# A two-layer hybrid decoder step on one core: a denser samples' chain, 64 expert blocks beside the gates instead of 72, and the last four expert blocks' products regrouped

## The chip, the cores and the metric

One core of one Trainium2 chip runs the whole program as a single launch. The metric is the device time of one execution in microseconds (us). Before the change the median of three runs is 3731.05 us (3728.86 to 3739.23).

## The reference, cut to what matters

Two trunk layers run over 512 prompt tokens (one sequence) and 64 sample tokens (8 sequences of 8), 1024 channels wide, in float32. Each layer has a mixer (a projection to 6 x 1024 columns, a gated recurrence, a short convolution, an output projection) and then an expert stage, in which every token takes 8 heads x 16 experts out of 16384.

```python
def trunk_layer(x, c, ...):
    sh1, sc1, g1, sh2, sc2, g2 = jnp.split(c @ w_ada + b_ada, 6, axis=-1)
    proj = modulate(rmsnorm(x, norm1), sh1, sc1) @ w_in
    ...
    merged = jax.nn.sigmoid(ga) * ya + jax.nn.sigmoid(gb) * yb
    x = x + g1[:, None, :] * (merged @ w_out)
    hn2 = modulate(rmsnorm(x, norm2), sh2, sc2)
    x = x + g2[:, None, :] * peer(hn2, ...)

def peer(...):                        # per block of tokens
    s = jnp.einsum('thpd,hpkd->thpk', q, sub_keys)
    sv, si = lax.top_k(s, TOPK)
    ...                               # 16 x 16 candidates, top 16 again: idx, g
    act = jax.nn.gelu(jnp.einsum('thkd,td->thk', u_tab[idx], xb))
    return jnp.einsum('thk,thkd->td', g * act, v_tab[idx])
```

## The kernel before, in words

**Two ways through the experts.** The first 384 prompt tokens (`TD`) go dense: the kernel multiplies them with all 16384 rows of the u table and of the v table, in 128 blocks of 128 experts, with a gate matrix that is zero where a token did not choose an expert. The other 128 prompt tokens (two groups of 64) and the 64 samples go by gathers: one indirect load on POOL brings 128 table rows (512 KB) at a time, and VectorE (DVE) either takes a dot product (`udot`, L666) or adds a weighted row (`vsum`, L682). These gathers are tasks in a queue (`gtasks`), 130 for the samples and 259 for the prompt tokens in each layer. `pump(n)` (L157) takes n of them, as a running credit, and is called from the loops of the dense work; what is left after the last block is flushed at L1052.

**Every dense float32 product is split.** `split_blk` (L127) makes a high part on ScalarE (ACT, L132) and a low part on DVE (L133, `lo_...`), and TensorE (PE) does three products. The split tiles rotate through 4 buffers (`HIS`), the raw blocks of 512 KB through 6 (`RAWS`); loads are issued by SP.

**A layer's stages.**
- The mixer (`mixer_in`, L334) does 48 projections of 24 products (`pj`, L150). Beside each, `beside()` (L369) takes `SIDE` steps of the samples' chain: the 64 samples' own pass through the same mixer, the query and the top-16 choice, a generator (`samples`, L459) of 56 steps, 36 of which load 1 MB (`sa_...`, L475). In layer 0 it also takes one chunk of the conditioning (`ada`, 1 MB, `pm`). When the chain has ended, `beside` pumps `MPUMP` gathers a projection.
- The output projection (`po`), then the queries (`pq`, with the top-16 choices on DVE, 8 heads).
- `phase_a` (L926): the products of the u blocks 0 to `NA`-1 (`u_mm`, `pu`, L713, 24 of 384 columns a block), beside the 96 pieces of the gate matrix (`oh` L945 and `A` L950 on DVE, `pgm` L955 on PE, eviction on ACT, 24 stores to DRAM). Blocks below `NS_` spill their activations to DRAM, the last 16 stay on the chip. In layer 0 the conditioning of layer 1 (24 chunks) goes here too.
- `phase_b` (L992): the blocks from `NA` on first, each with its u product just ahead (`meet`, `UAHEAD` pairs early; the stage is called the meets here), then the 16 resident ones, then the spilled ones (called the rest). For each block the activations are multiplied with the gates, split, and 18 products of 512 columns go to six PSUM banks (`pvo`, L1016). Six copies to SBUF (`ys`, L1059), transposes (`pyt`, L1065) and the update of x end the layer.

Nobody writes the order of the instructions by hand: a scheduler with a timeline of its own lays them out, by the priorities that `tc.high_priority` and `tc.issue_after` give.

## Time and profile before

| what | value |
|---|---|
| median of 3 runs | 3731.05 us |
| the profiled execution | 3730.17 us, span 3728.4 us |
| PE / DVE / ACT / POOL busy | 94% / 79% / 40% / 30% |
| granted PE clock, mean | 0.96 |
| DMA | 1032.70 MB, mean 277 GB/s |
| instructions | 52710 |

Layer 0 runs to about 1932 us of the span and layer 1 from there to the end. The table of stretches further down (rows 2) is cut at the stage ends. Busy time of PE is an upper bound, since a matmul that waits in the pipeline counts as busy. The pace of the products is therefore taken from the distance between starts.

### The profile page before, as it was taken

The page shows a single profiled execution, that of the slowest core. Times are in us where ns is not written, and L with a number is a line of the kernel's source. Part 1 is how long each engine was busy: PE and PEld are TensorE (multiplying, and loading weights), DVE is VectorE, ACT ScalarE, POOL GpSimd, SP SyncE. Part 2 cuts the span into 40 slices and gives each one's busy share as a digit, 9 for nine tenths or more (in the row PEclk, how much of TensorE's full clock was granted, in tenths as well). Part 3 has the DMA queues.
Part 4 walks back from the last instruction along what each step waited for, and adds up shares of the span by engine and source line. Part 5 has one row for each costly group of instructions (what it writes and reads, how often), then busy time and mean ns, then how long its engine had stood idle before and what let it go on. Part 6 is the DMA issues. An engine that isn't in the chain of part 4 may idle for free.

```text
span 3728.4 us, 52710 instructions
## 1 busy us (share of the span) xinstructions
PE 3501.1 (94%) x18606; PEld 2910.8 (78%) x18606; DVE 2961.9 (79%) x6160; ACT 1481.8 (40%) x2027; POOL 1119.1 (30%) x830
## 2 busy tenths in 40 slices
PE   7999989989999999999959999899999999999996
PEld 4447768977789999988844576789987999998885
DVE  5338889998758888888873489899998788888887
ACT  3324343435553333333323344434456433333332
POOL 0001530052004444432320036200720355554422
PEclk9999989989999999999979999999987999999998
DMA  8775853479879999999856669524984899999994
GB/s 296 269 253 202 303 201 111 157 267 348 325 272 322 342 340 339 336 366 347 323 186 231 247 214 332 173 89 173 336 310 187 289 347 338 343 337 363 357 336 169
DMA packets 393449, 1032.70 MB, mean 277 GB/s; under 512 B 54240, under 2 KB 159840, under 8 KB 386400
## 3 DMA queue, kind: packets, MB, share of 16 engines
q1 hardware_dynamic: 267616, 554.28, 42.6%
q0 software_dynamic: 110592, 402.70, 29.8%
q10 hardware_dynamic: 14976, 72.36, 4.8%
q8 instruction: 146, 2.39, 0.2%
q14 instruction: 119, 0.97, 0.1%
HBM read 954.01 MB, written 75.15 MB: 276 GB/s over the span
## 4 chain that ended last, share of the span: by engine, by line
PE 59%; issue 17%; POOL 11%; DVE 6%; DMA 5%; ACT 2%; POOLq 0%; SPq 0%; ACTq 0%; DVEq 0%
PE pu L713 22%; PE pvo L1016 14%; PE pj L150 8%; PE pq L871 5%; POOL vrp L660 4%; POOL urp L660 4%; POOL urs L660 3%; PE po L150 2%; PE pgm L955 1%; DMA raw_wi<-in_win_dram 1%; DVE A L950 1%; DVE oh L945 1%; PE pm L186 1%; DMA vrp<-in_vtab_dram,gidx 1%; DMA raw_ada<-in_wada_dram 1%
## 5 line engine op out<-in xcount | busy, mean ns | idle before, releaser
L660 POOL DMA_INDIRECT urp<-in_utab_dram,gidx x256 | 370.8, 1448 | 558.1 <-DVE dot L666 435.2
L660 POOL DMA_INDIRECT vrp<-in_vtab_dram,gidx x256 | 352.5, 1377 | 491.9 <-DVE accp L682 457.6
L1016 PE MATMUL pvo<-hi_v,h2h 128*128 128x512 f32 x1536 | 485.4, 390 | 0.0
L1016 PE MATMUL pvo<-lo_v,h2h 128*128 128x512 f32 x1536 | 476.8, 389 | 0.0
L1016 PE MATMUL pvo<-hi_v,h2l 128*128 128x512 f32 x1536 | 461.7, 389 | 0.0
L660 POOL DMA_INDIRECT vrs<-in_vtab_dram,gidxs x128 | 217.8, 1702 | 789.1 <-DVE fid L786 373.4
L713 PE MATMUL pu<-h2h,hi_u 128*128 128x384 f32 x1152 | 397.7, 345 | 4.8 <-ACT hi_u L132 3.3
L713 PE MATMUL pu<-h2h,lo_u 128*128 128x384 f32 x1152 | 395.2, 343 | 2.3 <-DVE lo_u L133 2.3
L713 PE MATMUL pu<-h2l,hi_u 128*128 128x384 f32 x1152 | 395.7, 343 | 0.0
L660 POOL DMA_INDIRECT urs<-in_utab_dram,gidxs x128 | 171.8, 1342 | 670.2 <-issue 314.3
L133 DVE TENSOR_TENSOR lo_v<-raw_v,hi_v 128x1024 fp32r<-128x1024 f32 x256 | 312.9, 1222 | 54.9 <-ACT hi_v L132 48.0
L150 PE MATMUL pj<-hnh,hi_wi 128*128 128x512 f32 (+1 forms) x800 | 320.7, 402 | 33.2 <-ACT hi_wi L132 12.8
L1016 PEld LDWEIGHTS pvo<-lo_v,h2h 128*128 128x128 f32 x1536 | 288.3, 188 | 60.8
L1016 PEld LDWEIGHTS pvo<-hi_v,h2l 128*128 128x128 f32 x1536 | 288.3, 188 | 60.5
L682 DVE SCALAR_TENSOR_TENSOR accp<-vrp,dot,accp 128x1024 f32<-128x1024 f32 x252 | 322.7, 1280 | 12.0 <-DMA vrp<-in_vtab_dram,gidx 10.8
L1016 PEld LDWEIGHTS pvo<-hi_v,h2h 128*128 128x128 f32 x1536 | 287.3, 188 | 56.1
L150 PE MATMUL pj<-hnl,hi_wi 128*128 128x512 f32 (+1 forms) x800 | 314.6, 393 | 4.2 <-DVE hnl L281 4.2
L150 PE MATMUL pj<-hnh,lo_wi 128*128 128x512 f32 (+1 forms) x800 | 316.3, 396 | 1.9 <-DVE lo_wi L133 1.8
L666 DVE CUSTOM_DVE_ANT_0 urp<-urp,xt 128x1024 f32<-128x1024 f32 x256 | 306.0, 1219 | 1.7 <-DMA urp<-in_utab_dram,gidx 1.6
L713 PE MATMUL pu<-h2h,lo_ub 128*128 128x384 f32 x896 | 300.1, 335 | 0.0
L713 PE MATMUL pu<-h2h,hi_ub 128*128 128x384 f32 x896 | 299.9, 335 | 0.0
L713 PE MATMUL pu<-h2l,hi_ub 128*128 128x384 f32 x896 | 299.7, 334 | 0.0
(439 smaller groups left out, 7178.4 us busy)
## 6 DMA issues: line engine op xcount, KB each, us to landing
raw_v<-in_vtab_dram SPq DMA_DIRECT2D x256, 512.0 KB
raw_u<-in_uT_dram SPq DMA_DIRECT2D x144, 512.0 KB
raw_ub<-in_uT_dram SPq DMA_DIRECT2D x112, 512.0 KB
raw_wi<-in_win_dram SPq DMA_DIRECT2D x96, 512.0 KB
gd<-stg ACTq DMA_DIRECT2D x48, 1024.0 KB
gt<-gd SPq DMA_DIRECT2D x768, 64.0 KB
raw_ada<-in_wada_dram SPq DMA_DIRECT2D x86, 512.0 KB
ad<-ao ACTq DMA_DIRECT2D x56, 384.0 KB
```

The costliest lines, as they stand in the source:

```text
L133: anchor[0] = V.tensor_tensor(out=lo, in0=raw, in1=hi.bitcast(F32), op=ALU.subtract).ins
L150: PE.matmul(out[:, c0:c1], a[:, w], b[:, k, c0:c1], start=(k == 0 and a is hi and b is xh), stop=(k == KT - 1 and a is lo))
L186: PE.matmul(pm[j * 32:(j + 1) * 32, 0:256], c32[:, k, :], raw[k // 4][:, j * 256:(j + 1) * 256], start=(k < 4), stop=(k >= 4))
L660: G.indirect_dma_start(out=rt, out_offset=None, in_=tab, in_offset=bass.IndirectOffsetOnAxis(ap=self.gidx[:, g, h, k:k + 1], axis=0))
L666: V.tensor_tensor_reduce(out=ur, in0=ur, in1=self.xt[g], scale=1.0, scalar=0.0, op0=ALU.mult, op1=ALU.add, accum_out=self.dot[:, g, h, k:k ...
L682: V.scalar_tensor_tensor(out=self.acc[g], in0=vr, scalar=w, in1=self.acc[g], op0=ALU.mult, op1=ALU.add)
L713: ends[i] = PE.matmul(pu[:, 0:TD], a[:, w], b[:, 0:NT, k, :], start=(k == 0 and a is hi and b is h2h), stop=(k == KT - 1 and a is lo)).ins
L871: PE.matmul(pqs[:, t0 * P:t1 * P], a[:, w], b[:, t0:t1, k, :], start=(k == 0 and a is hi and b is h2h), stop=(k == KT - 1 and a is lo))
L945: V.tensor_tensor(out=o, in0=iota2.unsqueeze(1).to_broadcast([P, 2, P, 2]), in1=slot(t, a, c0), op=ALU.is_equal)
L950: V.tensor_tensor(out=A[:, z], in0=oh[0], in1=slot(t, 2 + z, c0), op=ALU.mult)
L955: PE.matmul(pgm[:, n * P:(n + 1) * P], oh[1][:, n // 2, :, n % 2], A[:, z, n // 2, :, n % 2], start=(z == 0), stop=(z == 1))
L1016: PE.matmul(pv[t][q], a[:, tk], b[:, q * 512:(q + 1) * 512], start=(n == 0 and a is wh and b is vh), stop=(n == P - 1 and a is wl))
```

## The change

Four constants change, and two pieces of code. `NA` goes from 72 to 64, so that 64 u blocks run beside the gates and 64 in the meets (the resident ones are now 48 to 63, and 24 pairs are spilled, not 28). `SIDE` goes from (3.0, 3.5) to (4.5, 6.0) steps a projection, `MPUMP` from 2.5 to 2.6, and `BPUMP` from 3.0 and 1.0 to 3.2 and 1.4 gathers a block. `beside` takes two chunks of the conditioning at a time; its added condition `c < KT - 0` always holds. The products of the last two pairs (four blocks) are held back and issued after the loop, one 128-token tile `t` after the other, each followed by its copy out; the last pair's weights go to a part of `h2h`/`h2l` that is free by then.

```diff
-NA = 72
+NA = 64
...
-SIDE = (3.0, 3.5)
-MPUMP, QRATE, ARATE, BPUMP = 2.5, 0.0, 0.3, (3.0, 1.0)
+SIDE = (4.5, 6.0)
+MPUMP, QRATE, ARATE, BPUMP = 2.6, 0.0, 0.3, (3.2, 1.4)
...
-            if todo:
-                ada(l, [todo.pop(0)])
+            for _ in range(2):
+                if todo:
+                    ada(l, [todo.pop(0)])
...
-            if steps[0] < -1.0:
+            if steps[0] < -1.0 and c < KT - 0:
                 pump(MPUMP)
...
+        whe, wle = (h_[:, 0, :, :].rearrange("p k t -> p (k t)") for h_ in (h2h, h2l))
+        held = []
...
-                wh, wl = (w_[:, u * TD:(u + 1) * TD] for w_ in (wht, wlt))
+                last = n == P // 2 - 1
+                wh, wl = (w_[:, u * TD:(u + 1) * TD] for w_ in ((whe, wle) if last else (wht, wlt)))
...
-                for t in range(NT):
-                    products(t, 2 * n + u, wh, wl, vh, vl)
+                if n >= P // 2 - 2:
+                    held.append((2 * n + u, wh, wl, vh, vl))
+                else:
+                    for t in range(NT):
+                        products(t, 2 * n + u, wh, wl, vh, vl)
...
         for t in range(NT):
+            for h_ in held:
+                products(t, *h_)
             yt = ys[:, t].rearrange("p k t -> p (k t)")
```

**Place 1, the end of layer 0.** DVE before, from the next layer's first split (`lo_wi1`) to the last sums of the gathers (`accp`, of `vrp` rows), the update from them (`pf`) and those of the dense tokens (`pyt`):

```order
L133 TENSOR_TENSOR lo_wi1_0_1_17299<-raw1_wi1_0_0_17208,hi_wi1_0_1_17298 128x1024
L682 SCALAR_TENSOR_TENSOR accp0_1_15561<-vrp0_1_2_11_16921,dot0_3953,accp0_1_15561 128x1024
L682 SCALAR_TENSOR_TENSOR accp0_1_15561<-vrp0_1_2_12_16924,dot0_3953,accp0_1_15561 128x1024
...
L682 SCALAR_TENSOR_TENSOR accp0_1_15561<-vrp0_1_3_15_16981,dot0_3953,accp0_1_15561 128x1024
L737 SCALAR_TENSOR_TENSOR x_66<-pf0_1_16984,mod0_168,x_66 128x64 x8
L224 TENSOR_REDUCE ss_67<-sq0_17002 128x128
L1068 SCALAR_TENSOR_TENSOR x_66<-pyt0_0_0_17007,mod0_168,x_66 128x128 x4
```

DVE with the change, around its last sum of layer 0 (`lo_v0_36` is the split of v block 36; the last block is 47):

```order
L683 SCALAR_TENSOR_TENSOR accp0_1_14503<-vrp0_1_3_14_15871,dot0_4003,accp0_1_14503 128x1024
L1053 TENSOR_TENSOR h2l_4000<-at0_32_16519,h2h_3999 128x384
L133 TENSOR_TENSOR lo_v0_35_16608<-raw1_v0_32_1_16579,hi_v0_35_16607 128x1024
L683 SCALAR_TENSOR_TENSOR accp0_1_14503<-vrp0_1_3_15_15903,dot0_4003,accp0_1_14503 128x1024
L1053 TENSOR_TENSOR h2l_4000<-at0_32_16519,h2h_3999 128x384
L133 TENSOR_TENSOR lo_v0_36_16637<-raw0_v0_32_2_16632,hi_v0_36_16636 128x1024
```

Before, 25 sums (18 in layer 1) stand behind the split of the last block; now there are none, and the last one stands twelve blocks earlier.

PE before, from the last product of the dense blocks on (`pf`, the gathered tokens' result; `pyt`, transposes; `pva1`, the sums of squares for the next layer):

```order
L1016 MATMUL pvo0_2_1_10454<-hi_v0_55_16887,h2l_3950 128x512
L734 MATMUL pf0_1_16984<-eye2_77,accp0_1_15561 128x64 x8
L1065 MATMUL pyt0_0_0_17007<-ident_72,ys0_17001 128x128 x4
L1065 MATMUL pyt0_0_1_17016<-ident_72,ys0_17001 128x128 x4
L1065 MATMUL pyt0_1_0_17028<-ident_72,ys0_17001 128x128 x4
```

PE with the change, the same end:

```order
L1020 MATMUL pvo0_2_1_10252<-lo_v0_45_16892,h2h_3999 128x512
L1075 MATMUL pyt0_0_0_16946<-ident_72,ys0_16916 128x128 x4
L1075 MATMUL pyt0_0_1_16955<-ident_72,ys0_16916 128x128 x4
L1020 MATMUL pvo0_2_0_10251<-hi_v0_45_16891,h2l_4000 128x512
...
L1020 MATMUL pvo0_2_1_10252<-hi_v0_47_16909,h2l_4000 128x512
L1075 MATMUL pyt0_1_0_16991<-ident_72,ys0_16916 128x128 x4
L1075 MATMUL pyt0_1_1_17000<-ident_72,ys0_16916 128x128 x4
L237 MATMUL pva1_0_17089<-sq0_16917,ones_79 128x128 x8
```

The transposes of the first tile now stand among the held products of the third, and `pf` is gone from the end.

**Place 2, the end of the gates in layer 0.** PE before, from the last gate product (`pgm`) to the first product of `phase_b` (`pu0_68` is u block 68):

```order
L955 LDWEIGHTS oh10_2_124_9756
L955 MATMUL pgm0_2_7_3_9764<-A0_2_124_9758,oh10_2_124_9756 128x128
L713 MATMUL pu0_68_10283<-h2h_3949,lo_u0_68_10280 128x384
...
L713 MATMUL pu0_75_10559<-h2h_3949,lo_ub0_75_10556 128x384
L1016 MATMUL pvo0_0_0_10449<-hi_v0_72_10614,h2h_3949 128x512
```

PE with the change:

```order
L956 LDWEIGHTS oh10_2_124_9603
L956 MATMUL pgm0_2_7_3_9608<-A0_2_124_9605,oh10_2_124_9603 128x128
L714 MATMUL pu0_59_10009<-h2l_4000,hi_u0_59_10005 128x384
...
L714 MATMUL pu0_67_10357<-h2h_3999,lo_ub0_67_10354 128x384
L1020 MATMUL pvo0_0_0_10247<-hi_v0_64_10412,h2h_3999 128x512
```

The gates begin behind u block 30 in both; they end in block 68 before and in block 59 now, so the stretch with the gates holds 38.5 blocks before and 29.9 now, and the stretch behind it 7.5 and 8.1. In layer 1 the gates run from block 43.0 to 70.4 before and from 42.2 to 62.4 now, with 6.7 behind them in both.

**Place 3, the chain's last matmuls in layer 0.** PE before (`spgs0_1` are the chain's last scores, `pj0_3_1` is projection 1 of channel tile 3):

```order
L150 MATMUL pj0_3_1_2199<-hnh0_334,hi_wi0_3_1_2195 128x512
L150 MATMUL pj0_3_1_2199<-hnl0_335,hi_wi0_3_1_2195 128x512
L150 MATMUL pj0_3_1_2199<-hnh0_334,lo_wi0_3_1_2196 128x512
L609 MATMUL spgs0_1_2031<-sks0_1_2029,sqt1_0_1953 64x128 x8
L150 MATMUL pj0_3_2_2251<-hnh0_334,hi_wi0_3_2_2247 128x512
```

PE with the change:

```order
L150 MATMUL pj0_2_1_1967<-hnh0_334,hi_wi0_2_1_1963 128x512
L150 MATMUL pj0_2_1_1967<-hnl0_335,hi_wi0_2_1_1963 128x512
L610 MATMUL spgs0_1_1799<-sks0_1_1797,sqt1_0_1721 64x128 x8
L150 MATMUL pj0_2_1_1967<-hnh0_334,lo_wi0_2_1_1964 128x512
L150 MATMUL pj0_2_2_2019<-hnh0_334,hi_wi0_2_2_2015 128x512
```

The chain's matmuls end behind projection 20.0 before and 14.0 now; in layer 1 behind 17.7 and 11.6.

## Rows read from the trace of the kernel before

**Rows 1.** The page: busy time of PE and DVE, and the chain by engine.

```profile
PE 3501.1 (94%) x18606; PEld 2910.8 (78%) x18606; DVE 2961.9 (79%) x6160; ACT 1481.8 (40%) x2027; POOL 1119.1 (30%) x830
...
PE 59%; issue 17%; POOL 11%; DVE 6%; DMA 5%; ACT 2%; POOLq 0%; SPq 0%; ACTq 0%; DVEq 0%
```

**Rows 2.** Stretches by stage; the first row names the columns.

```profile
core 0: us, PE busy (x) PEld busy (x) DVE busy (x) ACT busy (x) POOL busy (x), PEclk, DMA share, GB/s
40.00:303.00 263.00, 243.56 (x1261) 141.50 (x1262) 101.44 (x192) 84.81 (x134) 0.00 (x0) 0.95 0.74 260
303.00:487.00 184.00, 169.07 (x702) 133.59 (x698) 162.13 (x325) 77.41 (x102) 83.47 (x64) 0.96 0.74 256
...
543.00:669.00 126.00, 120.62 (x685) 99.28 (x686) 117.69 (x616) 52.12 (x93) 6.35 (x5) 0.97 0.30 103
...
808.00:1100.00 292.00, 271.95 (x2131) 227.80 (x2131) 231.13 (x480) 158.25 (x198) 43.69 (x35) 0.94 0.88 322
...
1132.00:1876.00 744.00, 744.00 (x3586) 652.95 (x3584) 620.91 (x808) 268.70 (x360) 313.84 (x239) 1.00 0.95 341
1876.00:1932.00 56.00, 16.22 (x84) 14.03 (x83) 41.99 (x65) 11.66 (x19) 19.33 (x25) 0.62 0.46 159
...
1928.00:2140.00 212.00, 193.34 (x870) 113.39 (x871) 90.60 (x169) 72.51 (x108) 0.00 (x0) 0.96 0.65 227
2140.00:2336.00 196.00, 183.71 (x786) 145.41 (x784) 176.76 (x346) 87.39 (x114) 95.18 (x69) 0.99 0.78 275
...
2394.00:2520.00 126.00, 121.24 (x690) 99.68 (x689) 118.54 (x618) 51.69 (x93) 6.03 (x5) 0.97 0.30 103
...
2695.00:2914.00 219.00, 203.30 (x1450) 173.57 (x1449) 193.82 (x430) 138.92 (x153) 27.73 (x20) 0.84 0.64 244
...
2941.00:3679.00 738.00, 738.00 (x3545) 646.79 (x3543) 616.23 (x799) 264.54 (x355) 361.48 (x239) 1.00 0.94 339
3679.00:3729.00 50.00, 16.07 (x79) 13.76 (x78) 35.16 (x70) 9.58 (x14) 7.38 (x6) 0.62 0.37 125
```

**Rows 3.** PE's waits at the end of layer 0: total us, times, longest.

```profile
PE pf L734 <- DVE accp L682: 28.9, 1, 28.9
```

**Rows 4.** PE's waits at the end of layer 1.

```profile
PE pf L734 <- DVE accp L682: 14.9, 1, 14.9
```

**Rows 5.** Timeline at the end of layer 0, PE: start, duration, operation, count.

```profile
1870.65 0.61 PE L1016 MATMUL pvo<-hi_v,h2h 128*128 128x512 f32 x2
...
1875.64 0.61 PE L1016 MATMUL pvo<-hi_v,h2l 128*128 128x512 f32 x2
1905.19 3.68 PE L734 MATMUL pf<-eye,accp 128*128 128x64 f32 x16 [28.94 <-DVE accp L682]
...
1931.52 0.58 PE L150 MATMUL pj<-hnl,hi_wi 128*128 128x256 f32 x1 [3.11 <-DVE hnl L281]
```

**Rows 6.** Timeline of DVE at the ends of layers 0 and 1, second tile's update.

```profile
1915.90 2.16 DVE L1068 SCALAR_TENSOR_TENSOR x<-pyt,mod,x 128x128 f32<-128x128 f32 x8 [0.24 <-PE pyt L1065]
...
3705.49 1.03 DVE L1068 SCALAR_TENSOR_TENSOR x<-pyt,mod,x 128x128 f32<-128x128 f32 x4
```

**Rows 7.** Timeline of PE behind the gates, u products 13 apart.

```profile
1101.69 0.33 PE L713 MATMUL pu<-h2l,hi_u 128*128 128x384 f32 x1
...
1103.94 0.33 PE L713 MATMUL pu<-h2h,lo_u 128*128 128x384 f32 x1
```

**Rows 8.** DVE by line in layer 1's gates: busy, mean ns, idle before and releasers.

```profile
L133 DVE TENSOR_TENSOR lo_u<-raw_u,hi_u 128x1024 fp32r<-128x1024 f32 x26 | 31.8, 1223 | 11.3 <-ACT hi_u L132 11.2
L682 DVE SCALAR_TENSOR_TENSOR accs<-vrs,dots,accs 128x1024 f32<-128x1024 f32 x19 | 24.3, 1278 | 0.0
```

**Rows 9.** SP's own waits from 40 to 303 us, longest two.

```profile
SPq L141 <- PE pm L186: 33.9, 16, 6.1
SPq L141 <- PE sa_wq L475: 29.2, 11, 14.1
```

## The prediction

> **What bounds the kernel now.** I read the page first, then the table by stage, the waits at the two layer ends, the timelines there, and DVE's lines beside the gates. The page gives PE 94% busy, but its chain puts only 59% on PE and 11% on POOL [rows 1]: somewhere the gathers set the pace. The table shows where. Both stretches of phase_b run PE at full clock without a gap, 744 and 738 us [rows 2]. That they also lose nothing in pace is worked out: 22 products of 512 columns start within 4.99 us, 0.227 us each [rows 5], and 13 products of 384 columns within 2.25 us, 0.173 us each [rows 7]. A block of phase_b then costs 18 x 0.227 = 4.08 us for its v products, a u block 24 x 0.173 = 4.15 us. Layer 0 has 128 x 4.08 + 52 x 4.15 = 738 us of them in those 744 us (76 u blocks stand ahead). So phase_b is bound by PE, with 239 gathers hidden in it at 341 GB/s.
>
> The other stages differ. At the layer ends PE is busy 16 of 56 and 16 of 50 us at a clock of 0.62 [rows 2]: it waits 28.9 us [rows 3] and 14.9 us [rows 4] for the last gathers' sums. The gates have DVE 88% busy in layer 1 (194 of 219 us); in layer 0 PE (272 of 292), DVE (231) and the DMA (0.88) are all near their limit. The gather part of the mixer has DVE at 162 of 184 and 177 of 196 us, and the queries at 118 and 119 of 126 [rows 2]. Beside the chain DVE is idle and PE busy at a loose pace (244 of 263 us, DMA 0.74).
>
> **The sum, part by part,** against the profiled 3730.2 us; the three runs' median is 0.9 us above that.
>
> *Layer ends.* The order shows no gather left behind the last block. The last product before starts at 1875.64 in a row of two, so it ends near 1876.1, and the next layer's projections run on at 1931.52 [rows 5]: 55.4 us. From the second tile's update at 1915.90 [rows 6] to there it is 15.6 us; with the change this update can follow the last product within about 1 us, since its copy out and transposes are no longer behind pf. That leaves 16.5 us, a gain of 39. In layer 1 it is 3679.0 to 3728.4, 49.4 us, against 22.9 us from 3705.49 on [rows 6] and 0.7 for the transposes: a gain of 26. Of each, some 4 us are the held products; the rest is the tail of gathers. Held blocks keep all four split buffers, so the next layer's second split waits for them; such a split needs 1.2 us of DVE [rows 8] while the third tile's products still run, and I cost it at nothing. If that cover is gone it is 2 to 3 us. **-65.**
>
> *Phase_b.* Eight more u blocks a layer stand in a stage without slack: 8 x 4.15 = 33.2, twice. The greater BPUMP changes nothing there: DVE's order holds 24 gathers per eight blocks in the meets, before and now, so the load per block stays what 341 GB/s carried. **+66.**
>
> *Phase_a.* It gives up the same 33.2 us of PE, if PE set its pace. In layer 1's gates PE does not: 7.2 blocks fewer take away 7.2 splits of 1.22 us and 0.4 us of wait each [rows 8], 11.7 us, one gather of 1.28 is added, and 0.8 block (3.3 us) leaves the stretch before: 13.7 us less by DVE, 33 at most; I take 15. In layer 0, 8.6 blocks take 36 us off PE, 9 splits and 2 gathers 13.5 us off DVE, and some 6% off the DMA. With all three near the limit I take 25 of the 292 us, between 13 and 36, and 2.5 go back to the longer stretch behind the gates. **-22.5 and -15**, bounds -11 to -33 and -7 to -33.
>
> [...]
>
> *The mixer.* The chain's matmuls end six projections earlier, 14.0 for 20.0 and 11.6 for 17.7. Those projections move from beside the chain, where they cost PE 24 x 0.227 = 5.44 us, to beside the gathers, where one takes 184/28.0 = 6.57 us and 196/30.3 = 6.47 us [rows 2]. With the chain's own waits unchanged that is 6 x 1.13 and 6.1 x 1.03: **+13**. The order keeps 2 to 4 gathers a projection as before, so MPUMP is not felt. This supposes that the first stretch shrinks from 263 to 230 us and from 212 to 179, so its 65 and 45 MB must move at 284 and 253 GB/s, where 260 and 227 were seen. The chain's work tiles and the two chunks at once are in this; they add no bytes.
>
> *Output projection and queries.* 5 and 9 more sums of the samples' gathers stand behind the first wq split, in a stage with DVE 93% busy. Between nothing and 1.28 us each (6 and 12) I take two thirds: **+4, +8**.
>
> Sum: -65 + 66 - 37.5 + 13 + 12 = -11.5: 3730.2 - 11.5 = **3719 us**. In short: two waits go, and the stages that take up the work give most of it back.
>
> **The rivals.** A measurement of this kernel can tell about 0.3% (11 us) from no change, and the forecast lies right at that edge.
>
> *The chain keeps its pace (slower).* The chain's loads go through six raw buffers, and SP waits for PE to release them: 33.9 us for pm, 29.2 for the query chunks [rows 9]. If a denser chain only waits more for its own matmuls, the loads go on at 260 and 227 GB/s [rows 2]: 65.4/0.260 = 251 us for 230, 45.2/0.227 = 199 for 179. That is 41 us more: 3760 us. It decides from about 23 us on, that is once the first stretches together last over 432 us. For it: DMA 0.65 to 0.74 with PE never idle for long, so it is the turn of the buffers that limits; against: chunks and sample products free a buffer sooner than a projection does. Chance 0.15.
>
> *Cold gates (slower).* Layer 1's gates have PE busy 203 us at 0.84; less 30 us it is 173. If the clock falls under 173 x 0.84/207 = 0.70, PE sets the stage, and likewise layer 0 under 236 x 0.94/267 = 0.83. With both gates as long as before, phase_a gives back 1 us and not 37.5: 3755 us. Chance 0.09.
>
> *Gathers paid in full.* The 40 gathers that move to the mixer and the stages behind it cost their 1.28 us each, 51 us and not 25, but PE's waits there cover part of it; half the difference puts it at 3732 us, no change. DVE at 88% and 90% speaks for it, POOL idle 70% of the span against any wait of its own. Chance 0.09.
>
> *The denser chain uses the idle DMA (faster).* At phase_b's 341 GB/s the first stretches would need 192 and 132 us. A third of the way from 230 and 179 towards that is 13 and 16 us: 3690 us, and with half the way 3680. For it: 0.26 of the DMA lies idle there. Chance 0.20.
>
> That the change does not do what it says is true of two parts alone (BPUMP in the meets, the condition on c), and they are at zero above.
>
> **How the numbers follow.** The forecast has 0.47 and, with its bounds of some 20 us either way mostly in phase_a, lies on the faster side for 0.27 and within 0.3% for 0.20. Faster: 0.27 + 0.20 = 0.47. Slower: 0.14 of the first rival, 0.08 of the second, 0.02 of the third, 0.24. Same: the rest, 0.29. The range reaches down to 3684, past the faster rival's price, and up to 3756, to the cold gates and short of the chain's full price; the forecast's own is 3700 to 3738.
>
> **What would show it.** Right: no long wait of pf on accp at either layer end, and 14 to 20 us from the last dense product to the next layer's projections; phase_b some 33 us longer in each layer, still gapless; the gates 20 to 30 us shorter in layer 0 and about 12 in layer 1; the chain's last scores some 33 us earlier in each layer (near 270 us in layer 0); the queries 4 to 8 us longer. Wrong: waits of PE in phase_b, first stretches of the mixers over 240 and 190 us, or gates that did not shrink with a clock under 0.8.

## The result and the profile after

The changed kernel takes 3775.93 us (median of 4 runs, 3771.25 to 3781.93), the kernel before 3733.99 us (4 runs, 3728.86 to 3739.23). The ratio is 1.0113 with an interval of 1.0091 to 1.0135: slower by 1.1%, where I had forecast 3719 us and faster, and outside my range (3684 to 3756).

The page of the changed kernel, busy time and the chain by engine:

```profile
PE 3516.9 (93%) x18606; PEld 2924.6 (77%) x18606; DVE 2965.1 (79%) x6160; ACT 1484.9 (39%) x2027; POOL 1081.5 (29%) x830
...
PE 74%; DVE 7%; issue 6%; DMA 5%; POOL 5%; ACT 1%; SPq 0%; POOLq 0%; DVEq 0%; ACTq 0%
```

Beside [rows 1] this looks like success: the chain has moved from POOL (11%, now 5%) to PE (59%, now 74%). The gathers set the pace less than before, and yet the kernel is slower. The table by stretch says where, cut at the same stage ends as [rows 2]:

```profile
core 0: us, PE busy (x) PEld busy (x) DVE busy (x) ACT busy (x) POOL busy (x), PEclk, DMA share, GB/s
42.00:291.00 249.00, 205.71 (x1099) 114.08 (x1098) 82.64 (x167) 67.45 (x110) 0.00 (x0) 0.92 0.72 258
291.00:508.00 217.00, 200.48 (x845) 159.16 (x843) 192.82 (x367) 93.90 (x123) 101.62 (x75) 0.98 0.75 261
...
837.00:1115.50 278.50, 246.84 (x1945) 201.06 (x1945) 219.49 (x483) 148.41 (x181) 40.02 (x33) 0.86 0.84 311
...
1149.50:1928.00 778.50, 778.50 (x3786) 687.29 (x3786) 636.21 (x813) 283.61 (x382) 315.71 (x233) 1.00 0.91 328
1928.00:1945.00 17.00, 8.70 (x58) 7.92 (x56) 12.87 (x29) 7.50 (x13) 1.30 (x10) 0.84 0.16 48
1945.00:2146.50 201.50, 171.42 (x755) 93.37 (x755) 70.23 (x135) 55.21 (x81) 0.00 (x0) 0.89 0.65 229
2146.50:2370.00 223.50, 212.25 (x898) 168.59 (x898) 208.51 (x386) 106.51 (x139) 114.00 (x81) 0.99 0.78 273
...
2738.00:2946.00 208.00, 178.96 (x1274) 147.55 (x1273) 187.57 (x444) 127.78 (x138) 25.22 (x24) 0.76 0.63 240
...
2973.00:3753.00 780.00, 776.40 (x3764) 684.81 (x3763) 622.55 (x792) 280.67 (x380) 301.36 (x223) 1.00 0.87 315
3753.00:3775.00 22.00, 8.33 (x55) 7.67 (x53) 18.05 (x44) 5.59 (x8) 0.00 (x0) 0.79 0.34 108
```

Read it from the ends back. The layer ends are 17 and 22 us for 56 and 50. Both stretches of phase_b are longer. The gates (837 and 2738 us) are shorter, at a lower clock (0.86 and 0.76 for 0.94 and 0.84). And the two halves of each mixer, 249 and 217, 201.5 and 223.5 us, sum to more than before. To compare stage by stage I take the ends from PE's own products: first projection, the chain's last scores (`spgs`), first product of the output projection, of the queries and of the gates, last gate product, first and last v product. The forecast's terms stand beside them.

| stage, us | layer 0 before | after | layer 1 before | after | difference, both | forecast |
|---|---|---|---|---|---|---|
| mixer beside the chain | 263.4 | 249.0 | 218.0 | 205.2 | -27.2 | |
| rest of the mixer | 184.3 | 218.4 | 190.9 | 224.6 | +67.8 | |
| the mixer, both | | | | | +40.6 | +13 |
| output projection | 60.6 | 66.5 | 62.3 | 73.7 | +17.3 | |
| queries to the gates | 259.9 | 261.5 | 296.0 | 293.6 | -0.8 | +12 with the line above |
| gates | 292.3 | 278.4 | 218.1 | 207.4 | -24.6 | |
| behind the gates | 31.7 | 34.0 | 28.0 | 27.8 | +2.1 | -37.5 with the line above |
| phase_b | 744.1 | 778.6 | 737.9 | 779.5 | +76.1 | +66 |
| layer end | 51.6 | 13.2 | 49.2 | 22.4 | -65.2 | -65 |

With 1.8 us at the start that is 3728.4 + 47.1 = 3775.5, the span. Against the forecast's -11.5 some 59 us are missing: 28 in the mixer, 15 in the gates, 10 in phase_b, 4 in the output projection and the rest in small pieces.

**The layer end, as forecast.** The timeline of PE at the end of layer 0, the counterpart of [rows 5]:

```profile
1927.45 0.62 PE L1020 MATMUL pvo<-hi_v,h2l 128*128 128x512 f32 x2
1927.91 1.04 PE L1075 MATMUL pyt<-ident,ys 128*128 128x128 f32 x8
1928.78 1.95 PE L237 MATMUL pva<-sq,ones 128*128 128x128 f32 x16
...
1941.30 0.51 PE L150 MATMUL pj<-hnh,hi_wi 128*128 128x256 f32 x2 [0.99 <-ACT hnh L280]
```

No `pf` waits for `accp` there any more [rows 3, 4]; the transposes follow the last product at once, and the next layer's first projection comes 13 us behind it.

**The place where the mixer lost its gain.** Two pieces of PE's timeline in layer 0's first stretch. First the chain's recurrence gates (`spg`), then the way from the chain's output projection (`spt_wo`, its transposes) by the norm (`pvbs`) to the query products (`sa_wq`):

```profile
86.10 0.41 PE L537 MATMUL spg<-sxc,rg 128*128 128x64 f32 x2 [0.99 <-DMA rg<-in_rgwx_dram]
87.35 0.41 PE L537 MATMUL spg<-sxc,rg 128*128 128x64 f32 x2 [0.85 <-DMA rg<-in_rgwa_dram]
88.53 0.41 PE L537 MATMUL spg<-sxc,rg 128*128 128x64 f32 x2 [0.78 <-DMA rg<-in_rgwx_dram]
...
228.00 0.60 PE L483 MATMUL spt_wo<-ident,tm_wo 128*128 128x128 f32 x4
238.24 0.69 PE L237 MATMUL pvbs<-ss,ones 128*128 128x64 f32 x2 [9.65 <-DVE ss L224]
242.17 3.68 PE L650 MATMUL pxts<-ident,sh 128*64 128x128 f32 x32 [3.24 <-DVE sh L273]
245.64 4.94 PE L476 MATMUL sa_wq<-raw_s_wq,sh 128*64 128x512 f32 x20
```

The same way in the kernel before:

```profile
235.08 1.05 PE L482 MATMUL spt_wo<-ident,tm_wo 128*128 128x128 f32 x4
235.79 0.78 PE L150 MATMUL pj<-hnh,lo_wi 128*128 128x512 f32 x1
...
245.34 0.33 PE L237 MATMUL pvbs<-ss,ones 128*128 128x64 f32 x2
245.48 0.47 PE L150 MATMUL pj<-hnh,lo_wi 128*128 128x512 f32 x1
```

Before, 10 us also lie between `spt_wo` and `pvbs`, but they are filled with projections (`pj`). In the changed kernel PE stands still for 9.65 and 3.24 us. At the recurrence gates it crawls: 24 small products in the 14.7 us from 84.7 to 99.4, each pair waiting for two small loads. What the loads do meanwhile, by the transfers of the changed kernel from 84 to 100 us:

```profile
DMA packets 2003, 0.43 MB, mean 27 GB/s; under 512 B 2002, under 2 KB 2002, under 8 KB 2002
```

and by SP's two largest waits in the whole first stretch (total us, times, longest):

```profile
SPq L141 <- PE sa_wq L476: 40.7, 16, 21.8
SPq L141 <- PE pm L186: 26.6, 19, 5.9
```

SP's own timeline shows what it issued at the two places:

```profile
84.58 1.18 SPq L364 DMA_DIRECT2D rg<-in_rgwa_dram  x2
85.86 1.18 SPq L364 DMA_DIRECT2D rg<-in_rgwx_dram  x2
...
216.78 8.56 SPq L141 DMA_DIRECT2D raw_s_wq<-in_swq_dram  x6
247.19 1.19 SPq L141 DMA_DIRECT2D raw_s_wq<-in_swq_dram  x2
```

and in the kernel before, ahead of the same norm:

```profile
228.34 2.46 SPq L141 DMA_DIRECT2D raw_wi<-in_win_dram  x2
```

What the two places have in common stands in PE's order: the chain can't go on, and no projection stands there that PE could do instead. What holds the chain up differs. At the recurrence gates it is SP's queue: the small loads (`rg`, 16 KB each) are issued in one row, one every 0.64 us, 0.43 MB in 16 us, and a pair of products needs two of them. At the norm it is DVE, and there the raw buffers are full of the chain's own next loads: six blocks of the query chunks are issued by 225.3 us, and the seventh goes out at 247.19, when PE has released one. That is SP's wait of 21.8 us in one piece (14.1 before, [rows 9]). In the kernel before, two of the blocks loaded ahead of the norm were a projection's (`raw_wi`). PE's waits at `spg`, `pvbs` and `pxts` together are 20.9 us in layer 0's first stretch, and 2.7 in the kernel before.

### The profile page after: what moved, and what is told of

Read it like the earlier page. It is cut to its first block, busy times and chain, and to the rows that moved or that the text cites. A ratio compares the mean times of both kernels' runs of the same rounds, so it can differ in the third digit from the quotient of the medians.

```text
span 3775.5 us, 52702 instructions
## 1 busy us (share of the span) xinstructions
PE 3516.9 (93%) x18606; PEld 2924.6 (77%) x18606; DVE 2965.1 (79%) x6160; ACT 1484.9 (39%) x2027; POOL 1081.5 (29%) x830
## 4 chain that ended last, share of the span: by engine, by line
PE 74%; DVE 7%; issue 6%; DMA 5%; POOL 5%; ACT 1%; SPq 0%; POOLq 0%; DVEq 0%; ACTq 0%
PE pvo L1020 27%; PE pu L714 27%; PE pj L150 5%; PE pq L872 5%; POOL urs L661 4%; POOL vrs L661 2%; DVE A L951 2%; DVE oh L946 1%; PE pgm L956 1%; DMA vrs<-in_vtab_dram,gidxs 1%; DMA raw_wi<-in_win_dram 1%; PE po L150 1%; PE pm L186 1%; PE pd L886 1%; DVE accs L683 1%
## 5 line engine op out<-in xcount | busy, mean ns | idle before, releaser
L661 POOL DMA_INDIRECT urp<-in_utab_dram,gidx x256 | 341.6, 1334 | 712.7 <-DVE dot L667 497.7
L661 POOL DMA_INDIRECT vrp<-in_vtab_dram,gidx x256 | 341.9, 1336 | 460.7 <-DVE accp L683 425.4
L714 PE MATMUL pu<-h2h,hi_u 128*128 128x384 f32 x1024 | 352.4, 344 | 3.4 <-ACT hi_u L132 3.3
L714 PE MATMUL pu<-h2h,lo_u 128*128 128x384 f32 x1024 | 350.3, 342 | 0.3 <-DVE lo_u L133 0.3
L714 PE MATMUL pu<-h2l,hi_u 128*128 128x384 f32 x1024 | 349.9, 342 | 0.0
L714 PE MATMUL pu<-h2h,hi_ub 128*128 128x384 f32 x1024 | 343.5, 335 | 0.0
L714 PE MATMUL pu<-h2h,lo_ub 128*128 128x384 f32 x1024 | 343.2, 335 | 0.0
L714 PE MATMUL pu<-h2l,hi_ub 128*128 128x384 f32 x1024 | 343.0, 335 | 0.0
```

The lines of the kernel that those rows point to most:

```text
L661: G.indirect_dma_start(out=rt, out_offset=None, in_=tab, in_offset=bass.IndirectOffsetOnAxis(ap=self.gidx[:, g, h, k:k + 1], axis=0))
L714: ends[i] = PE.matmul(pu[:, 0:TD], a[:, w], b[:, 0:NT, k, :], start=(k == 0 and a is hi and b is h2h), stop=(k == KT - 1 and a is lo)).ins
```

## The experiments

I held two theories of the long first stretch against each other all along: that the loads through six buffers have a rate that they keep (the slow rival of the prediction), and that PE stands idle at the chain's serial places, that is where a step of the chain must wait for the one before it. Line numbers in rows of the experiments are shifted by a few lines against the kernel before.

**half_chain.** Half of the chain's weight loads are left out.

```diff
-                raw = load_pair(src[kk], f"s{l}_{nm}_{kk}")
+                raw = [st.tile([P, D], F32, tag="raw", bufs=RAWS, name=f"raw0_s{l}_{nm}_{kk}")] * 2
+                with tc.high_priority(offset=AHEAD):
+                    SY.dma_start(raw[0], src[kk][:, 0, :])
```

> The changed kernel, but each step of the samples' chain loads one raw block of 512 KB and uses it for both halves, so half of the chain's weights are left out; its matmuls and its dependent steps stay. Theory A (the stretch beside the chain goes at the pace at which raw blocks are loaded and their buffers come free): it shrinks from 249 to under 200 us in layer 0 and from 203 to under 165 us in layer 1, and the whole by 60 us or more. Theory B (the chain's dependent steps set it): both stretches stay within 12 us of 249 and 203.

Measured: 3723.24 us (one run). The two first stretches of this kernel, by the table of stretches:

```profile
42.00:269.50 227.50, 205.43 (x1101) 119.08 (x1101) 82.14 (x166) 66.63 (x109) 0.00 (x0) 0.91 0.60 201
1922.00:2094.00 172.00, 162.65 (x775) 96.04 (x775) 71.77 (x156) 57.97 (x86) 0.00 (x0) 0.94 0.48 160
```

227.5 and 172 us lie between the expectations, so neither theory stands alone. The rate is no constant either: 201 and 160 GB/s where 258 and 229 were moved. Fewer chain loads also leave buffers free for projections, so this run could not tell the theories apart; the runs with empty steps below could.

**chain_undone, na_undone and held_only: each part alone.** chain_undone is the changed kernel with the chain as before; na_undone has 72 blocks beside the gates again; held_only is the kernel before with nothing but the held products and the new `BPUMP`.

```diff
# chain_undone, against the changed kernel
-SIDE = (4.5, 6.0)
-MPUMP, QRATE, ARATE, BPUMP = 2.6, 0.0, 0.3, (3.2, 1.4)
+SIDE = (3.0, 3.5)
+MPUMP, QRATE, ARATE, BPUMP = 2.5, 0.0, 0.3, (3.2, 1.4)
...
-            for _ in range(2):
-                if todo:
-                    ada(l, [todo.pop(0)])
+            if todo:
+                ada(l, [todo.pop(0)])
# na_undone, against the changed kernel
-NA = 64
+NA = 72
```

> The changed kernel with the samples' chain as before (3.0 and 3.5 steps, one chunk at a time, MPUMP 2.5); NA 64, BPUMP and the held blocks stay. Theory A (the denser chain costs the mixers some 41 us and the output projections 17): mixers back to 447 and 408 us, 3720 us or a little more, since the order leaves some 10 gathers behind the last block of layer 0 (13 us). Theory C (the loss is NA 64 alone): the mixers change by less than 10 us each, 3765 us.

> The changed kernel with NA 72; the denser chain, BPUMP and the held blocks stay. Theory A: phase_b gets some 70 us shorter in the two layers together, phase_a only 25 longer, a short tail of 5 gathers (7 us) comes back in layer 0: 3735 to 3745 us. Theory D (phase_a shrank by all that phase_b grew): within 8 us of 3776.

> The kernel before with the held blocks and the greater BPUMP alone. If the gathers' places are set by what fits and not by BPUMP, the order keeps the tail (25 and 18 gathers behind the last block) and only the held products gain, some 4 us a layer: 3722 to 3732 us. If BPUMP draws gathers forward, both waits of pf go and it is under 3700 us.

Measured: chain_undone 3719.63 us, ratio to the kernel before 0.9950 (0.9934 to 0.9967). na_undone 3725.33 us, 0.9971 (0.9956 to 0.9987). held_only 3732.92 us, 0.9992 (0.9982 to 1.0002). chain_undone came out as its theory A had it, with mixers of 450.7 and 412.8 us. na_undone is 10 us under theory A's band: phase_b is 73.3 us shorter than in the changed kernel and the gates 20.9 longer, and the layer ends only 2 us longer. held_only is 1 us over its band for a tail that stays. The spans of the profiled executions make a square:

| span, us | 72 blocks | 64 blocks |
|---|---|---|
| chain as before | 3734.2 (held_only) | 3720.6 (chain_undone) |
| denser chain | 3719.2 (na_undone) | 3775.5 (the change) |

By these spans each part alone gains 14 to 15 us, and the two together lose 41. By the medians the parts gain 13 (64 blocks) and 8 us (the denser chain), since na_undone's profiled execution was the fastest of eight. If they added, the change would stand at 3705.6, so 70 us belong to their meeting (64 by the medians). Some 49 of these are in the layer ends: 101.3 us of both layers with neither part, 49.8 and 37.7 with one, 35.6 with both, where the sum of the two gains would be -13.8. Either part takes away most of the one tail of gathers, and the second pays its price, here 55 or 56 us, for what is left. Another 12 of the 70 us are in layer 0's gates. held_only shows that `BPUMP` and the held products shorten nothing in sum while the tail stands (ends of 56.0 and 45.3 us for 51.6 and 49.2).

**no_held.** The last four blocks' products are not held back.

```diff
-                if n >= P // 2 - 2:
+                if n >= P // 2 + 2:
                     held.append((2 * n + u, wh, wl, vh, vl))
```

> The changed kernel with the last four blocks' products not held back: each block's products follow it, and the copies out and transposes come after the last. My sum had some 4 us for the held products in each layer's end. Theory A (they are worth that): layer ends of 13 and 22 become 15 to 20 and 24 to 29, the time 3780 to 3790. Theory B (holding costs the next splits their buffers, or phase_b a wait, as much as it gives): the time within 4 us of the changed kernel's 3776, and phase_b of layer 1 some 2 to 7 us shorter.

Measured: 3781.69 us, ratio to the kernel before 1.0129 (1.0112 to 1.0146). The layer ends are 14.9 and 27.0 us for 13.2 and 22.4, phase_b 777.6 and 780.3 for 778.6 and 779.5. Theory A has the sign; the price is 1.7 and 4.6 us, not 4 twice.

**spread: the same work, dealt out otherwise.**

```diff
-SIDE = (4.5, 6.0)
+SIDE = (6.0, 8.0)
...
                 PE.matmul(pgs[m][:, c * NS:(c + 1) * NS], rgs[c % 2][m], xc[:, c, :], start=True, stop=True)
+            yield 1
...
         norm_samples(h2, *scales(mx, mod, vt[:, O_N2:O_N2 + KT], 3, f"bs{l}"))
-        yield 1
+        for _ in range(12 if l == 0 else 16):
+            yield 1
```

> The changed kernel with the same number of projections beside the chain, but dealt out otherwise: eight empty steps of the chain between its recurrence-gate products (one after each channel tile), 11 (layer 0) and 15 (layer 1) empty steps between the chain's output projection and its query products, and SIDE raised to 6.0 and 8.0 so that the chain still ends behind projection 14.0 (11.9 in layer 1). No load and no product is added or taken away. Theory A (the first stretch is long because at two serial places of the chain, the recurrence gates and the norm ahead of the query products, the six raw buffers hold the chain's next loads and no projection is left for PE): PE's idle at spt_wo, pvbs and spg goes, some 27 us in layer 0 and 16 in layer 1 of the changed kernel; first stretches of 249 and 205 become 225 to 235 and 188 to 195, the time 3730 to 3750. Theory B (the rate of the loads through six buffers sets it, whatever the order): 258 and 229 GB/s stay, stretches 243 to 255 and 200 to 210, the time 3765 to 3785.

Measured: 3751.79 us, ratio to the kernel before 1.0050 (1.0033 to 1.0067), so 24 us below the changed kernel and just above theory A's band. Layer 0's first stretch is 230.3 us, in the middle of theory A's band; layer 1's is 204.1, in theory B's. The trace of layer 1 tells why. Its way to the query products is filled now, but eight empty steps at 8.0 steps a projection are a single projection, and its recurrence gates stood in one row, 24 products from 1960.2 to 1975.0 us. PE's waits of spread from 1960 to 1976 us:

```profile
PE spg L537 <- DMA rg<-in_rgwx_dram: 4.4, 6, 1.0
PE spg L537 <- DMA rg<-in_rgwa_dram: 3.8, 6, 1.1
```

So one serial place had been exchanged for the other, or so theory A would have it. That could be tried.

**spread_l1.** Layer 1's recurrence gates are dealt out as well.

```diff
-SIDE = (6.0, 8.0)
+SIDE = (6.0, 12.0)
...
-            yield 1
+            for _ in range(1 if l == 0 else 4):
+                yield 1
...
-        for _ in range(12 if l == 0 else 16):
+        for _ in range(12 if l == 0 else 24):
```

> The run spread with layer 1's recurrence gates dealt out as well: in that run the eight channel tiles' gate products of layer 1 still stood in one row (24 products in 15.7 us, PE waiting for each pair of small loads), since eight empty steps at SIDE 8.0 are one projection. Now 32 empty steps there, 24 ahead of the queries, and SIDE 12.0 in layer 1, with the chain ending behind projection 11.7 as before; layer 0 is as in the run spread. Theory A (the two serial places hold layer 1's first stretch up too, and the run spread had only exchanged one for the other): the first stretch of layer 1 becomes 186 to 195 for 204, the time 3734 to 3745. Theory B (in layer 1 the rate of the loads sets it, as the run half_chain with 172 us would have it): 200 to 208, the time 3747 to 3757.

Measured: 3737.69 us (10 runs), ratio to the kernel before 1.0002 (0.9993 to 1.0012). Layer 1's first stretch is 182.8 us, some 3 us under theory A's band, layer 0's 227.4. Both, by the table of stretches:

```profile
42.80:270.10 227.30, 202.92 (x1103) 110.14 (x1099) 81.90 (x167) 71.38 (x113) 0.00 (x0) 0.96 0.80 285
1921.20:2104.00 182.80, 162.49 (x759) 90.70 (x759) 76.50 (x148) 62.15 (x92) 0.00 (x0) 0.95 0.70 252
```

And layer 1's way past the norm in PE's timeline, where rows of projections lie between these two:

```profile
2047.70 0.60 PE L483 MATMUL spt_wo<-ident,tm_wo 128*128 128x128 f32 x4
...
2056.35 0.33 PE L237 MATMUL pvbs<-ss,ones 128*128 128x64 f32 x2
```

This decides it. The chain still ends behind projections 14.0 and 11.7, the loads and products are the same, the six buffers too, and the same bytes go at 285 and 252 GB/s where the changed kernel had 258 and 229. The rate followed from the order; it did not set it. Each first stretch is 22 us shorter than the changed kernel's, and PE's waits at `spg`, `pvbs` and `pxts` fell from 20.9 to 2.2 us in layer 0 and from 16.7 to 2.9 in layer 1. So 19 and 14 of the 22 us are those waits themselves; the rest I did not place. Whether more raw buffers would have let the projections through without a new order was not tried.

**denser_ada4.** A chain denser still (the conditioning four chunks at a time, so that it is there when the chain needs it).

```diff
-SIDE = (4.5, 6.0)
+SIDE = (9.0, 12.0)
...
-            for _ in range(2):
+            for _ in range(4):
```

> The changed kernel with SIDE 9.0 and 12.0 and four conditioning chunks at a time: the chain's matmuls end behind projections 8.0 and 7.7 (14.0 and 11.6 in the changed kernel), so 6.0 and 3.9 projections more go out of the first stretch. Theory A (the chain's serial places set the stretch, and a projection taken out leaves PE idle there): stretches of 235 to 249 and 195 to 205; the rest of the mixer some 39 and 25 us longer; the time over 3810. Theory B (the rate of the loads, 258 and 229 GB/s): the 6.3 and 4.1 MB that leave make 24 and 18 us, stretches of 225 and 187; the time 3785 to 3805. The forecast's own rule (5.44 us for each projection that leaves): 216 and 184, the time about 3775.

Measured: 3787.67 us (2 runs), ratio to the kernel before 1.0132 (1.0111 to 1.0152). First stretches of 219.7 and 183.8 us, 29 and 21 less than the changed kernel's; the rest of the mixers +35 and +17. With two chunks at a time a chain of this density would read conditioning that isn't written yet, so that form has no time. My theory A, as I had put it, falls here: taking out six and four projections more did shorten the stretches, by nearly the 5.44 us each of the forecast's rule. Stretches and time are close to theory B's, but not for its reason: the bytes went at 279 and 239 GB/s, not at 258 and 229. What stays of theory A is narrower. With 8.0 and 7.7 projections left the stretches are no more than 8 us shorter in layer 0, and no shorter at all in layer 1, than spread_l1's with 14.0 and 11.7. So six and four projections fit beside the chain almost for nothing, if they stand where the chain waits.

**no_low_part: what sets the gates.**

```diff
-                    hi, lo = split_blk(raw[u], f"u{l}_{i}")
+                    hi = lo = high_blk(raw[u], f"u{l}_{i}")
```

(`high_blk` is `split_blk` without DVE's subtraction; the products' `start` and `stop` go by their count.)

> The changed kernel without the low part of the u blocks that run beside the gates: DVE's subtraction is left out for the blocks 0 to 63 (PE multiplies the high part in its place, so its 24 products a block stay). That takes 1.22 us a block off DVE, some 30 blocks in layer 0's gates and 20 in layer 1's, and nothing off PE or the DMA. Theory A (with eight blocks fewer the gates are set by DVE's one-hot and gate pieces, for which PE waited 22 and 26 us): 278 and 207 us become 245 to 262 and 180 to 190. Theory B (PE at its lower clock of 0.86 and 0.76, or the DMA, sets them): both stay within 6 us, or the clock falls no further and PE's waits only change their name.

Measured: 3691.02 us (one run). The two stretches of gates, by the table of stretches:

```profile
806.60:1058.20 251.60, 236.31 (x1920) 194.74 (x1920) 176.09 (x440) 147.23 (x180) 30.18 (x28) 0.93 0.87 323
2642.10:2862.20 220.10, 211.99 (x1577) 187.86 (x1576) 163.91 (x421) 142.89 (x163) 23.65 (x23) 0.91 0.70 266
```

Layer 0's gates fall from 278 to 252 us, inside theory A's band, and by PE's order with 31.2 u blocks in them, not 29.9. Layer 1's rise to 220 us, outside both bands, because the order changed: the gates begin behind block 28 and not 42, and hold 33.6 blocks, not 20.2. Counted from the queries to the last gate product, layer 1 has 461.6 us for 501.0. In both layers the clock rises, from 0.86 to 0.93 and from 0.76 to 0.91, and PE's wait for DVE's gate pieces (`A`) falls, from 22.1 to 9.6 us and from 25.8 to 6.8. In layer 1, with so many more blocks in the stretch, the two clocks are not of like work.

**old_spread, spread_72 and spread_72_l1old: is there a better kernel?** The square says to pay for the tail once, the runs with empty steps how. old_spread is chain_undone with the empty steps; the other two have the denser chain with the empty steps and 72 blocks beside the gates, the last one with layer 1's chain at its old density.

```diff
# old_spread, against chain_undone: the empty steps of spread, and
-SIDE = (3.0, 3.5)
+SIDE = (4.0, 4.9)
# spread_72, against spread
-NA = 64
+NA = 72
# spread_72_l1old, against spread_72
-SIDE = (6.0, 8.0)
+SIDE = (6.0, 4.9)
```

> The kernel of the run chain_undone (64 blocks beside the gates, held blocks, the chain at its old density, one conditioning chunk at a time) with the same empty steps at the two serial places and SIDE 4.0 and 4.9, so that the chain ends behind projections 20.0 and 18.4 (20.0 and 17.7 before). Theory A (serial places without a projection): in the kernel before PE's holes of over 1.5 us in these stretches were 18 and 17 us in all, few of them at the serial places, so there is less to gain than with the denser chain: first stretches of 266 and 218 become 255 to 262 and 210 to 218, the time 3705 to 3717. Theory B (rate of the loads): 266 and 218 stay within 4, the time 3716 to 3724.

> The run spread with 72 blocks beside the gates again (both parts that were found to pay for each other's gain: the chain dense but dealt out, and eight u blocks fewer in phase_b). Theory A (the stages add, as long as only one of the two takes the tail of gathers away): the run na_undone had 3725.3 us; the first stretch of layer 0 becomes 230 for 249 as in the run spread, that of layer 1 stays near 201, the output projections give 1 to 3 us: 3703, between 3697 and 3709. Theory B (what the first stretch gives is taken back by the gates and the layer end, since 12 and 5 gathers stand behind the last eight blocks' splits): 3712 to 3725.

> The run before this one with layer 1's chain at its old density (SIDE 4.9 with the empty steps; it ends behind projection 18.4, not 11.7). Theory A (the stages add): layer 1's mixer and output projection take 465 us as in the run old_spread, where na_undone had 499, so 34 us less; 23 gathers stand behind the last eight splits of phase_b there, and the layer end goes from 23 to 38 to 46; in sum 3684 to 3698. Theory B (gathers taken out of the mixer cost in the tail what they cost there, about 1.4 us each, 20 of them): 3698 to 3712, the same as the run before this one within 5 us.

Measured: old_spread 3718.45 us, 0.9954 (0.9939 to 0.9970). Its first stretches, 264.6 and 216.2 us, are within 3 us of chain_undone's, as theory B had it; after spread_l1 I read this as serial places that were covered already at the old density. spread_72 3698.23 us, 0.9884 (0.9865 to 0.9904), as the stages' sum had it (3703). spread_72_l1old **3679.26 us, 0.9849 (0.9832 to 0.9865)**, 59 us below the kernel before in the runs beside it (3738.28), the best of the study and under the range of theory A (3684 to 3698). Its table of stretches, layer 0's first stretch, gates, phase_b and end, then layer 1's mixer and end:

```profile
41.00:272.40 231.40, 208.33 (x1099) 114.41 (x1098) 80.88 (x165) 71.01 (x111) 0.00 (x0) 0.93 0.78 279
...
819.70:1097.50 277.80, 261.26 (x2146) 221.47 (x2146) 228.52 (x493) 159.71 (x199) 38.47 (x33) 0.98 0.91 334
1130.00:1874.00 744.00, 744.00 (x3586) 652.93 (x3584) 623.30 (x798) 270.67 (x365) 311.98 (x234) 1.00 0.94 340
1874.00:1889.00 15.00, 9.71 (x63) 8.51 (x61) 11.38 (x31) 6.92 (x10) 1.00 (x7) 0.89 0.11 38
1889.00:2107.70 218.70, 200.30 (x924) 119.40 (x924) 95.82 (x174) 75.88 (x113) 0.31 (x4) 0.98 0.66 228
2107.70:2286.10 178.40, 171.71 (x731) 136.62 (x731) 167.55 (x333) 83.57 (x110) 89.97 (x66) 1.00 0.76 275
...
3633.30:3671.00 37.70, 16.49 (x78) 14.07 (x78) 27.36 (x64) 9.47 (x14) 0.00 (x0) 0.62 0.23 79
```

phase_b is as short as before (744 us), layer 0's end is 15 us for 52, the first stretch 231 for 263. Layer 1's gathers do better in a tail of 38 us than in the mixer of spread_72, whose layer 1 still has its gates in one row. The rival was not tried: spread_72 with those gates dealt out as in spread_l1 would gain some 22 us by that run's stretch, which puts its span near 3680 as well (an estimate, 3702.2 less 22). Two gains in it I did not take apart: layer 0's gates are 278 us at 72 blocks, where na_undone had 286.5, and layer 1's rest of the mixer is 178 us where chain_undone had 194, of which the chain's later end (projection 18.4 for 17.7, at the 6.47 us a projection of the kernel before) explains some 4.5, by estimate.

## Why the prediction was wrong

**The step that failed is the mixer's**, and in it one clause: "With the chain's own waits unchanged that is 6 x 1.13 and 6.1 x 1.03". The waits did not stay. Six projections left each first stretch, and it should have gone to 230 and 179 us; it went to 249 and 205. (The 179 start from a stretch cut at 2140 us, 5.9 us ahead of the chain's last scores; by the ends of the table above it is 218 less 33, so 185.) A good part of the six had been what PE did while the chain's recurrence gates and its norm had nothing for it. With projections put back at those two places, and no other work changed, the stretches are 227 and 183 us and the two mixers together 0.2 us longer than before (448.2 and 408.6 for 447.7 and 408.9), where the forecast had +13. So the price of a projection and the shrinking were about right; the cover was not checked at the places where it was needed, though PE's order with the change told of them (in layer 0 `spt_wo`, `pvbs` and the first query products stand without a projection between them) and PE's timeline of the kernel before showed the projections standing there.

**The slow rival was right in its numbers and not in its cause.** "The chain keeps its pace" gave 251 and 199 us, "41 us more", and a total of 3760; measured were 249 and 205. But it had the loads keep 260 and 227 GB/s because of the turn of the buffers, and spread_l1 moves the same loads through the same buffers at 285 and 252. A rate read from a stretch with holes in it is a mean over the holes. It took "PE never idle for long" as a sign that the turn of the buffers limits; that was true of the order before (PE's longest wait in layer 0's first stretch is 4.1 us) and not of the one after (9.6 us). I gave this rival 0.15.

**The gates** gave back 24.6 us (22.5 with the stretch behind them), not 37.5. I had bounded layer 0 by DVE's 13.5 and PE's 36 us and taken 25; it is 13.9, at DVE's end of the bounds. Layer 1 gave 10.7, where I had worked out 13.7 by DVE and taken 15. PE's wait in layer 0 for DVE's pieces, among its waits in layer 0's gates (total us, times, longest), in the kernel before

```profile
PE pgm L955 <- DVE A L950: 9.2, 11, 2.0
```

and in the changed kernel

```profile
PE pgm L956 <- DVE A L951: 22.1, 18, 2.8
```

The blocks taken away beside the gates came back in part as this wait for DVE's gate pieces. In layer 1 the size holds in every pair of runs that differs by the eight blocks alone: 12.6 us (held_only, chain_undone), 12.8 (na_undone, the change) and 13.3 (spread_72, spread). In layer 0 the same pairs give 20.1, 8.1 and 1.6 us (289.0 and 268.9, 286.5 and 278.4, 277.6 and 276.0), so what the blocks are worth there hangs on the rest of the order, and what sets those gates stays open. The granted clock fell from 0.94 to 0.86 and from 0.84 to 0.76, as the cold-gates rival had it, and short of what that rival needed in either layer (0.83 and 0.70). In both layers PE waited longer for the gate pieces, 22.1 us for 9.2 and 25.8 for 12.8. no_low_part took only DVE work away, and in layer 0 PE's wait for the gate pieces fell from 22.1 to 9.6 us and the clock came back to 0.93: the low clock there went with PE's waits for DVE. What the clock adds on top was not measured alone.

**phase_b** cost 34.5 us in layer 0 (33.2 forecast) and 41.6 in layer 1. The 8 us more there have a new wait that I had not foreseen. `pf` of the first group stands in mid-stream, before and now; in layer 1 it now waits for its sum, at 3419.5 us, while the u products queue behind it:

```profile
PE pf L735 <- DVE accp L683: 3.6, 1, 3.6
```

Behind it the u products start 0.32 us apart, and 0.173 again only from 3424.6 us on, with a granted clock of 0.82 from 3423 to 3427. chain_undone has no such wait and 774.2 us, so these two go with the denser chain and make about 5 of the 8 us. The other 3 are in chain_undone too: there, as in the changed kernel, 16 more products of `pf` and ten transposes stand inside the stretch than before.

**The output projection**, +17.3 us with nothing at the queries, where I had +12 for both: the gathers moved ahead cost it, not the queries. DVE has 19 and 23 operations of the samples' gathers in that stage, 16 and 15 before, and the stage is as long with the denser chain alone (67.0 and 71.4 us in na_undone, 59.4 and 64.1 in held_only). In layer 1 PE waits 9.6 us in one piece there for `ss` of DVE. The **layer ends** came out at -38.4 and -26.8 for -39 and -26, though the held products are 1.7 and 4.6 us of that and not 4 each.

With the mixer mended the change is still worth nothing (spread_l1, at the kernel before's time, is that case). The square shows what the sum did not ask. It counted the tail once, which was right, and the cost of both parts against it; it never asked what either part would be worth alone.

## What to carry to other kernels

Work that looks merely interleaved may be the cover of a serial place: before you take it out, find in the timeline what PE does in each wait of the other chain, and leave enough there; a mean rate or a mean price over the stretch doesn't show it. Where two changes pay for the removal of the same tail, try each alone first, since the second buys only what the first has left. And when a stage with two engines near their limit loses work on one, start from the other engine's bound, not from the middle: in layer 1's gates that was 13.7 us, and three pairs of runs gave 12.6 to 13.3.

## What the runs showed of the hardware that I had not expected

A row of small loads left the transfer side nearly idle. While the chain's recurrence weights came in, SP issued 16 KB loads one behind the other, each 0.59 us long and one every 0.64; 16 us passed with 0.43 MB moved (27 GB/s, a DMA share of 0.12, 2002 packets under 512 B), one pair of products came every 1.2 to 1.4 us, and the granted clock of those 16 us was 0.67. The size did not make these issues long: a 512 KB load of the kernel before (a query block at 226.43 us) took SP 0.33 us. The clock of a stretch also rose when only VectorE's work was taken out: layer 0's gates in no_low_part have as many products a block, on 31.2 blocks for 29.9, and stood at 0.93 where they were 0.86.
